# ifftshift of an 8192 x 8192 matrix: copies as pairs of half rows instead of blocks of half rows

## The chip, the cores and the metric

The kernel runs on one core of one Trainium2 chip. The metric is the device time of one execution in microseconds (us), lower is better; the figure for a kernel is the median of its runs.

## The reference

```python
def setup_inputs():
    return {"x": np.random.randn(8192, 8192).astype(np.float32)}

def reference(x):
    return np.fft.ifftshift(x)
```

For even sizes this swaps the halves of both axes: output row r, left half, is input row (r + 4096) mod 8192, right half; output row r, right half, is the left half of the same input row. Nothing is computed. 268.44 MB (8192 x 8192 x 4 bytes) are read and as many are written.

## The kernel before

Input and output lie in DRAM, and each transfer goes from the one straight to the other; no on-chip memory and no compute engine takes part. A row is 32 KB (R = C = 8192, float32), half a row 16 KB; `hr` and `hc` are 4096.

The helper `copy` (L26) starts one transfer on a queue (L29). Its list `dims` holds step and count of each dimension and is used for both sides, so source and destination have the same shape; the source is the destination shifted by half the rows and half the columns. The first dimension, of size 16, is divided over the 16 DMA engines.

There are two queues. SP (`nc.sync`) copies the left halves of output rows, ACT (`nc.scalar`) the right halves. Rows are taken in blocks of `rows` = 256: one transfer is 256 half rows, 4 MB. The shape `back` (L45) gives each engine one of 16 neighbouring rows, and its next piece lies 16 rows earlier, so engine e takes rows e + 240, e + 224, and so on down to e of the block. The loop (L47) goes from the last 1024 rows to the first, four blocks at a time in descending order; in the same step ACT works two blocks (512 rows, 16 MB) away from SP.

Ahead of the loop ACT copies one band of 16 half rows, the last of its first block, in strips of 1024 columns (4 KB pieces, L36 to L42): three strips are each divided into a transfer of 14, 9 or 4 rows and one of the rest, the fourth is one transfer of 16 rows. ACT's first block leaves this band out (`rest`, 240 half rows).

In all 71 transfers: 32 on SP, 39 on ACT. Their order on each queue is the program's. Eight semaphores serve in turn for the completion of all transfers, so the issue of a transfer waits until the one that had its semaphore has landed.

Of the kernel before, what the change touches and what calls it, by code (L numbers as in the profile page):

```python
# [1 line left out]

# [4 lines left out]


ENGINES = 16


@with_exitstack
def kernel(
    ctx: ExitStack,
    tc: tile.TileContext,
    x: bass.AP,
    out: bass.AP,
):
    nc = tc.nc
    R, C = x.shape  # L20
    hr = R // 2
    hc = C // 2
    per = 16
    rows = ENGINES * per

    def copy(queue, row, col, dims):  # L26

        src = (row + hr) % R * C + (col + hc) % C
        queue.dma_start(  # L29
            out=bass.AP(out.tensor, out.offset + row * C + col, dims),  # L30
            in_=bass.AP(x.tensor, x.offset + src, dims),
        )

    start = R - 3 * rows  # L36
    strip = hc // 4
    for n, k in enumerate((14, 9, 4)):
        col = hc + n * strip
        copy(nc.scalar, start + rows - ENGINES, col, [[C, k], [1, strip]])  # L40
        copy(nc.scalar, start + rows - ENGINES + k, col, [[C, ENGINES - k], [1, strip]])
    copy(nc.scalar, start + rows - ENGINES, hc + 3 * strip, [[C, ENGINES], [1, strip]])  # L42


    back = [[C, ENGINES], [-ENGINES * C, per], [1, hc]]  # L45
    rest = [[C, ENGINES], [-ENGINES * C, per - 1], [1, hc]]
    for first in range(R - 4 * rows, -1, -4 * rows):  # L47
        for n in (3, 2, 1, 0):
            copy(nc.sync, first + n * rows + rows - ENGINES, 0, back)
            right = first + (n + 2) % 4 * rows  # L50
            if right == start:
                copy(nc.scalar, right + rows - 2 * ENGINES, hc, rest)
            else:
                copy(nc.scalar, right + rows - ENGINES, hc, back)


# [1 line left out]
_INS = ['x']  # L58
_OUTS = [((8192, 8192), 'float32')]


# [23 lines left out]
```

## Time and profile before

| | |
|---|---|
| median of 3 runs | 821.84 us (821.51 to 823.76) |
| profiled execution: span from first to last instruction | 810.9 us |
| profiled execution: its own total | not given by the page; the median is 10.9 us over the span |
| copied | 268.44 MB, mean 331 GB/s; read and written 662 GB/s |
| packets | 17,520, of which 1,152 are under 8 KB |
| transfers on SP | 32 of 4096 KB |
| transfers on ACT | 31 of 4096 KB, 1 of 3840 KB, 7 strips of 8 to 64 KB |
| issue of one transfer on its queue | 571 ns (SP), 578 ns (ACT), medians |

How to read it: the page has a row for the busy share of the 16 DMA engines in 40 equal slices and one for the rate in each (GB/s counts bytes copied once; memory sees each twice). A packet is one piece of a transfer on one engine. q1 is SP's queue and q10 ACT's. The compute engines do nothing but four small constants at the start, so the chain of waits, which follows instructions, says nothing about this kernel; what there is to see is in the DMA rows.

### The profile page before, as it was taken

What the parts mean: (1) busy time and instruction counts of PE and PEld (TensorE: products, weight loads), DVE (VectorE), ACT (ScalarE), POOL (GpSimd) and SP (SyncE); (2) the same over time, 40 slices, a digit from 0 to 9 for tenths busy, and PEclk for the clock granted to TensorE, in tenths of its full rate; (3) what the DMA queues carried; (4) which work ended last, traced back from release to release, by engine and by line L of the source; (5) the groups of instructions that cost most, each with busy time, mean ns of one, the idle gap of its engine ahead of it and who ended that gap; (6) DMA issues with size and microseconds to landing.
All of it is one profiled execution on the core that took longest, in us unless ns stands there. A gap on an engine that the chain in (4) does not pass through costs nothing. (4 is left out here: it accounts for less than half of the span.)

```text
span 810.9 us, 116 instructions
## 1 busy us (share of the span) xinstructions
POOL 0.2 (0%) x4
## 2 busy tenths in 40 slices
POOL 0000000000000000000000000000000000000000
DMA  9999999999999999999999999999999999999998
GB/s 302 328 335 329 334 333 331 331 335 330 326 331 329 331 335 330 332 332 337 335 336 333 333 337 330 334 335 331 336 331 333 335 334 335 333 330 336 333 338 296
DMA packets 17520, 268.44 MB, mean 331 GB/s; under 512 B 1088, under 2 KB 1088, under 8 KB 1152
## 3 DMA queue, kind: packets, MB, share of 16 engines
q1 hardware_dynamic: 8704, 134.22, 49.7%
q10 hardware_dynamic: 8816, 134.22, 49.6%
HBM read 268.44 MB, written 268.44 MB: 662 GB/s over the span
## 5 line engine op out<-in xcount | busy, mean ns | idle before, releaser
L69 POOL MEMSET const-bfloat16-1.0<- 128x1 bf16 x1 | 0.1, 102 | 0.0
L69 POOL MEMSET const-uint8-127<- 128x1 uint8 x1 | 0.1, 102 | 0.0
L69 POOL MEMSET const-float32-0.0<- 128x1 f32 x1 | 0.1, 99 | 0.2 <-issue 0.2
L69 POOL MEMSET const-float32-1.0<- 128x1 f32 x1 | 0.1, 99 | 0.0
## 6 DMA issues: line engine op xcount, KB each, us to landing
out_dram<-in_x_dram SPq DMA_DIRECT2D x32, 4096.0 KB, 100.9
out_dram<-in_x_dram ACTq DMA_DIRECT2D x31, 4096.0 KB
out_dram<-in_x_dram ACTq DMA_DIRECT2D x1, 3840.0 KB
out_dram<-in_x_dram ACTq DMA_DIRECT2D x1, 64.0 KB, 10.8
out_dram<-in_x_dram ACTq DMA_DIRECT2D x1, 56.0 KB
out_dram<-in_x_dram ACTq DMA_DIRECT2D x1, 48.0 KB
out_dram<-in_x_dram ACTq DMA_DIRECT2D x1, 36.0 KB
out_dram<-in_x_dram ACTq DMA_DIRECT2D x1, 28.0 KB
```

The costliest lines, as they stand in the source:

```text
L69: nc = _bacc.Bacc("TRN2", target_bir_lowering=False, num_devices=1)
```

## The change

The left half of an output row comes from the right half of an input row, and the left half of the next input row goes to the right half of the next output row. In the input these two halves lie next to each other. `pair_copy` copies n such pairs: the source is one contiguous run of n x 32 KB that starts in the middle of input row k, and the destination is, for each pair, the left half of output row k + 4096 and the right half of the row below it. Of 256 pairs each of the 16 engines gets 16, 512 KB of the input in one run, written in pieces of 16 KB. Rows ascend.

SP copies the pairs that start in input rows 0 to 4095, ACT those of rows 4096 to 8191. The last pairs of each half would wrap around; so each queue starts with a shorter transfer of 240 pairs (rows 3840 to 4079 of its half) and three small ones by `half_copy`: 16 left halves, 15 right halves and one right half. Then 15 transfers of 256 pairs (8 MB) follow on each queue. That makes 38 transfers in place of 71. Strips, descending order and the distance of two blocks between the queues go.

```diff
-    def copy(queue, row, col, dims):
+    def pair_copy(queue, k, n):
+        to = (k + hr) % R
+        queue.dma_start(
+            out=bass.AP(out.tensor, out.offset + to * C, [[C, n], [C + hc, 2], [1, hc]]),
+            in_=bass.AP(x.tensor, x.offset + k * C + hc, [[C, n], [1, C]]),
+        )
 
+    def half_copy(queue, row, col, n):
         src = (row + hr) % R * C + (col + hc) % C
         queue.dma_start(
-            out=bass.AP(out.tensor, out.offset + row * C + col, dims),
-            in_=bass.AP(x.tensor, x.offset + src, dims),
+            out=bass.AP(out.tensor, out.offset + row * C + col, [[C, n], [1, hc]]),
+            in_=bass.AP(x.tensor, x.offset + src, [[C, n], [1, hc]]),
         )
 
+    full = hr // pairs - 1
+    last = full * pairs
+    n = hr - ENGINES - last
+    for queue, base in ((nc.sync, 0), (nc.scalar, hr)):
+        pair_copy(queue, base + last, n)
-    start = R - 3 * rows
-    ...
-    back = [[C, ENGINES], [-ENGINES * C, per], [1, hc]]
-    rest = [[C, ENGINES], [-ENGINES * C, per - 1], [1, hc]]
-    for first in range(R - 4 * rows, -1, -4 * rows):
-        ...
+        k = base + last + n
+        to = (k + hr) % R
+        half_copy(queue, to, 0, ENGINES)
+        half_copy(queue, to + 1, hc, ENGINES - 1)
+        half_copy(queue, (base + hr) % R, hc, 1)
+    for i in range(full):
+        pair_copy(nc.sync, i * pairs, pairs)
+        pair_copy(nc.scalar, hr + i * pairs, pairs)
```

(`pairs` is 256, as `rows` was.)

More of the change, by code (lines that the diff above doesn't have):

```diff
@@ L23 @@
     per = 16
-    rows = ENGINES * per
-    def copy(queue, row, col, dims):
+    pairs = ENGINES * per
+    def pair_copy(queue, k, n):
[5 more added lines that the diff above has]
+    def half_copy(queue, row, col, n):
         src = (row + hr) % R * C + (col + hc) % C
         queue.dma_start(
-            out=bass.AP(out.tensor, out.offset + row * C + col, dims),
-            in_=bass.AP(x.tensor, x.offset + src, dims),
-        )
-    start = R - 3 * rows
[L37 to L42, printed above, removed]
-    back = [[C, ENGINES], [-ENGINES * C, per], [1, hc]]
-    rest = [[C, ENGINES], [-ENGINES * C, per - 1], [1, hc]]
-    for first in range(R - 4 * rows, -1, -4 * rows):
[L48 to L54, printed above, removed]
+            out=bass.AP(out.tensor, out.offset + row * C + col, [[C, n], [1, hc]]),
+            in_=bass.AP(x.tensor, x.offset + src, [[C, n], [1, hc]]),
+        )
+    full = hr // pairs - 1
[11 more added lines that the diff above has]
+        pair_copy(nc.scalar, hr + i * pairs, pairs)
 _INS = ['x']
```

## The prediction

> **What bounds the kernel now.** The kernel has no arithmetic: it is 71 transfers from one DRAM tensor to another. So I read, in this order, the slices of the page, the DMA queues, the waits of the queue SP, and then my own table of stretches.
>
> The page first. The row DMA is the busy share of the 16 DMA engines in tenths for each fortieth of the span (20.3 us), and GB/s is what they copied.
>
> ```profile
> DMA  9999999999999999999999999999999999999998
> GB/s 302 328 335 329 334 333 331 331 335 330 326 331 329 331 335 330 332 332 337 335 336 333 333 337 330 334 335 331 336 331 333 335 334 335 333 330 336 333 338 296
> DMA packets 17520, 268.44 MB, mean 331 GB/s; under 512 B 1088, under 2 KB 1088, under 8 KB 1152
> q1 hardware_dynamic: 8704, 134.22, 49.7%
> q10 hardware_dynamic: 8816, 134.22, 49.6%
> HBM read 268.44 MB, written 268.44 MB: 662 GB/s over the span
> ```
>
> The engines are never free between head and tail: the two queues (q1 and q10, 134.22 MB each) fill 99.3% of them. So the time is packets x time per packet / 16. Of q1's 8,704 packets 512 are the completion marks of its 32 transfers (16 each, 9 ns apiece), so 8,192 carry 16 KB, and each takes 0.497 x 16 x 810.9 us / 8,192 = 787 ns. The single packet records say the same (mean 786, median 725), and they have a floor: the shortest is 608 ns, and 35% end within 620. An engine alone would thus need 608; the other 179 ns of the mean is waiting on memory, in some packets and not in others. That is the only thing this change can move: no byte goes away.
>
> Next, whether issuing or waiting costs anything. In the waits of the queue SP the columns are total us, times and longest us.
>
> ```profile
> SPq L29 <- DMA out_dram<-in_x_dram: 686.8, 28, 28.4
> SPq L80 <- DMA out_dram<-in_x_dram: 103.2, 3, 83.6
> out_dram<-in_x_dram SPq DMA_DIRECT2D x32, 4096.0 KB, 100.9
> ```
>
> SP waits nearly all the time, but for a completion mark of a transfer four back: a 4 MB transfer lands 100.9 us after its issue, which is 8 of them in flight (8 x 4.19 MB / 331 GB/s = 101 us). The rings hold work while SP waits, so the wait costs nothing.
>
> Last, the stretches (columns: window, its us, POOL, clock, DMA share, GB/s).
>
> ```profile
> 0.00:2.30 2.30, 0.20 (x4) 1.00 0.26 64
> 2.30:8.00 5.70, 0.00 (x0) 1.00 1.00 356
> 8.00:19.00 11.00, 0.00 (x0) 1.00 0.98 322
> 19.00:21.50 2.50, 0.00 (x0) 1.00 1.05 315
> 55.00:400.00 345.00, 0.00 (x0) 1.00 1.00 331
> 400.00:780.00 380.00, 0.00 (x0) 1.00 1.00 334
> 806.00:811.00 5.00, 0.00 (x0) 1.00 0.48 167
> ```
>
> From 2.3 to 8 us nearly all traffic is SP's and goes at 356; once both queues mix it is 331 to 334. So with the engines full throughout, the rate still moves by 7% with which addresses are in flight together: that is the size of what is at stake here. Between 18.8 us (SP's first transfer has landed) and about 21 (its second, issued at 19.25, is moving) only ACT's ring has work, and the engines stay full: one queue covers the other.
>
> The span is 810.9 us; the page gives no total for its execution, and the median of the runs is 821.84. I take the 10.9 us between them as fixed work around the span and add it to every figure below. About 0.3% (2.5 us) is what can be told from no change.
>
> **The change, part by part.**
>
> *Fewer, larger transfers.* 71 issues become 38 (30 of 8 MB, two of 7.5 MB, six small). An issue takes 0.57 us on its queue, 18.8 us on SP in all, beside full rings: nothing, covered by the 8 transfers in flight. If the cover were missing it would be one issue, 0.6 us.
>
> *The head.* ACT's seven strip transfers go, whose 4 KB packets held ACT's first large transfer back until some 13 us. SP's ring covered that (356 GB/s), so nothing is gained there; the 2.3 us before the first traffic stay.
>
> *The seam near 50 us.* This is new. With eight completion marks shared in turn, as the waits of before show, the first large transfers have to wait for the two 7.5 MB ones. Those land together: 7.86 MB at half of 331 GB/s is 47.5 us, from 2.3 on, so at 50. Behind them each ring has only its small pieces, about 2 packets an engine and queue: 4 x 787 ns = 3.1 us of cover. Restarting takes 0.5 us from landing to issue (18.8 to 19.25 above) and about 1.6 from issue to traffic (0.73 to 2.3), together 2.1; the 16 engines' marks of one transfer are spread over 1.2 to 2.7 us, so an engine that ended early runs dry for up to 3.1 - 2.1 against that spread, some 0 to 1.7 us. Bounds 0 and 4 (no cover, both rings); I take 1.
>
> *The tail and the split.* Each queue still moves 134.22 MB. The 15-row piece gives one engine a packet less per queue, the one-row piece may give another one more: at most 2 x 787 ns = 1.6 us late at one engine. Before has the like (its strips give engine 0 28 KB and engine 15 4 KB). Bounds -1 and +1.6; I take 0, since packets shift between engines' ends by about as much anyway.
>
> *Read runs of 32 KB or more instead of 16.* If a packet's own overhead were what counts, it would be seen at the floor: 16,384 B in 608 ns is 26.9 GB/s; a 4 KB strip packet takes 159 ns at the least, 25.8 GB/s. From the two, the fixed part of a packet is 159 - (608 - 159) / 3 = 9 ns, 1.2%, and only a packet that is at the floor gains it. Bounds: 0, and the fixed part of every packet, 16,368 x 9 ns / 16 = 9 us to the good; I take 0, since the engine isn't what the mean waits for.
>
> *The addresses in flight.* This is the term that decides. Before, an engine takes half a row and steps back 16 rows; the 16 engines stand on 16 neighbouring rows, 32 KB apart. SP and ACT work 512 rows (16 MB) apart. After, an engine walks its own 16 rows and the engines stand 512 KB apart; SP reads input rows from k and writes output rows from k + 4096 while ACT reads from k + 4096 and writes from k, so all four streams stand at the same row within a half, where before SP's two and ACT's two were 16 MB from each other. For it: a read run covers whole rows, and the writes of two halves of one output row follow each other. Against it: wider equal strides and four streams in step. No row of the trace shows a stride of 512 KB between engines, so I bound it. Better end: the stretch at 356 GB/s. Worse end: the first packet of each of the 16 engines, which start in step, takes 974 ns in the mean against 786 (it holds first-access delay as well). The nearest rows are whole slices, where the mixture of addresses turns as the rows advance: 326 to 338 in the 38 inner slices. I take the slow end, 326, because of the strides and because two mixed queues already cost 7% against one: 810.9 x 331 / 326 = 823.3.
>
> The Trainium skill has a rule that speaks against this part: DMA: Bandwidth & Descriptors, section Latency and other measured facts, gives copies between DRAM tensors whose rows lie at large powers of two apart, 207 GB/s at 512 KiB against 214 unhampered, and 164 and 103 at wider pitches. By its 512 KiB row an estimate would be 810.9 x 214 / 207 = 838.3, so 850 in all instead of 835; its pitch is between neighbouring 16 KiB rows, here it is between engines, and no run yet shows which counts.
>
> Sum: 823.3 + 1 + 0 + 10.9 = **835 us**.
>
> **The rivals.**
>
> *Slower, forecast (0.43).* As summed; with slices of 331 and 322 GB/s as its limits, 825 to 845.
>
> *Faster (0.31).* The whole-row reads and the paired half-row writes find memory better: the packets between 620 and 1,000 ns go towards the floor. Place: every packet after 2.3 us. At the best inner slice, 338 GB/s: 810.9 x 331 / 338 = 794.1, + 11.9 = 806. At 356: 766. It decides as soon as the mean packet falls under 783 ns per 16 KB, half a per cent below now, more than the seam costs. For it: 179 ns of waiting per packet is there to win, and the head runs at 356. Against it: the engines wander apart by 1 to 3 us, so which rows neighbour in time is partly chance, and longer runs need not matter.
>
> A ceiling for this case stands in the Trainium skill, HBM Reference, Specifications: about 716 GB/s for a domain. Against the page's 662 it would allow an estimate of 810.9 x 662 / 716 = 749.7, 762 in all; the stretch at 356 (712 read and written) agrees with it.
>
> *No change (0.11).* The pattern doesn't matter, the engines' wandering mixes it in both kernels: 821.84 + 1 = 823, between 819.4 and 824.3.
>
> *Much slower (0.12).* The strides alias: engines and streams that hit the same part of memory hold each other up all the time, not in turns. Slowest 2 us piece of the head after the strips (14 to 16 us): 299 GB/s; 810.9 x 331 / 299 = 897.7, so 910; at 974 ns a packet 1,016. Against it: continuous rings let a delayed engine fall out of step.
>
> *The split isn't what it says (0.03).* A contiguous source could be cut over fewer than 16 engines. With 15 for all: 810.9 x 16 / 15 = 865, so 877; fewer give more.
>
> **How the numbers follow.** The likeliest case gives 835. The range is 798 to 885: it holds the forecast, no change and the split at 15; of the faster case it leaves out the part under 798 (about 0.08), of the two bad ones what lies above 885 (about 0.10). The forecast's own range is 825 to 845. Slower by over 0.3%: 0.43 + 0.12 + 0.03 = 0.58; same 0.11; faster 0.31.
>
> **What would show it.** Forecast right: the inner slices near 326 GB/s, DMA still all 9, the two queues' shares still near 49.7% each. Faster: slices of 335 and above, more packets near the floor. Seam: a dip in the slice of 40 to 61 us, and a DMA share under 1 near 50 us; if several us are lost there, my cover is wrong. Much slower: slices under 310. A split over fewer engines: the DMA share at or under 0.94. The prediction is wrong if the slices rise above 331, or fall under 310.

## The result and the profile after

The changed kernel takes 862.8 us (median of 4 runs, 861.92 to 865.76) against 821.67 for the kernel before (4 runs): a ratio of 1.050, 95% interval 1.047 to 1.054, or 41 us. The forecast was 835 us.

The page of the changed kernel, in the rows that were read before:

```profile
span 864.0 us, 83 instructions
...
DMA  9999999999999999999999999999999999999998
GB/s 291 315 315 313 312 306 313 310 320 313 309 313 313 314 303 309 317 307 313 310 306 315 319 314 313 306 312 318 316 304 313 312 313 313 315 307 313 318 315 272
DMA packets 17020, 268.44 MB, mean 311 GB/s; under 512 B 606, under 2 KB 638, under 8 KB 638
...
q1 hardware_dynamic: 8510, 134.22, 50.0%
q10 hardware_dynamic: 8510, 134.22, 49.4%
HBM read 268.44 MB, written 268.44 MB: 621 GB/s over the span
```

The engines are as full as before (nines in all slices but the last, the two queues 99.4%), so the source was not cut over fewer than 16 engines. But every inner slice is slow: 303 to 320 GB/s, where before had 326 to 338. The loss is spread evenly, so it isn't an event. The packets show that it is their length. 16,382 packets of 16 KB now last 838 ns in the mean against 786 (of 16,368): 838.4 x 16,382 / 16 - 786.5 x 16,368 / 16 = 54 us, which is the difference of the spans, 864.0 - 810.9 = 53. The floor is still 608 ns; only 27% of the packets end within 620 ns, 35% before. No packet grew: although the source is one unbroken run, each record still moves 16 KB.

One reading aid. In every later run the time is 1.7 to 2.0 us above its span (here 865.76 and 864.0). So the profiled execution of before, whose own time is not on record, probably took about 812.7 us, some 7 us less than the fastest timed run of that kernel. Of the 53 us between the two spans some 44 are the change's (865.8 against the median 821.7).

The stretches of the changed kernel (window, its us, POOL, clock, DMA share, GB/s), with the seam and the tail:

```profile
2.30:8.00 5.70, 0.00 (x0) 1.00 0.95 336
...
19.00:48.00 29.00, 0.00 (x0) 1.00 0.99 315
...
50.00:52.00 2.00, 0.00 (x0) 1.00 0.89 287
52.00:54.00 2.00, 0.00 (x0) 1.00 0.89 297
...
60.00:400.00 340.00, 0.00 (x0) 1.00 1.00 311
400.00:800.00 400.00, 0.00 (x0) 1.00 1.00 312
```

The waits of SP (total us, times, longest us) and the transfers (number, size, us to landing) show what stands behind the rows of 50 to 54 us:

```profile
SPq L31 <- DMA out_dram<-in_x_dram: 120.6, 15, 51.2
...
out_dram<-in_x_dram ACTq DMA_DIRECT2D x15, 8192.0 KB, 215.1
out_dram<-in_x_dram SPq DMA_DIRECT2D x15, 8192.0 KB, 214.8
out_dram<-in_x_dram ACTq DMA_DIRECT2D x1, 7680.0 KB, 50.1
out_dram<-in_x_dram SPq DMA_DIRECT2D x1, 7680.0 KB, 54.3
```

SP's longest wait is 51.2 us, for a transfer of 7.5 MB; from then on 8 transfers of 8 MB are in flight, and each lands 215 us after its issue (64 x 1.049 MB / 311 GB/s = 216). So the seam is there, but at a share of 0.89 it costs about 4 x 0.11 = 0.4 us. (Windows of 2 us scatter by about as much in the kernel before, 0.88 to 1.14, so this is a size and not a measurement.) The rest of the time simply passes at 311.

### The profile page after: what moved, and what is told of

It reads as the page before. It is cut to its first block, busy times and chain, and to the rows that moved or that the text cites. A ratio compares the mean times of both kernels' runs of the same rounds, so it can differ in the third digit from the quotient of the medians.

```text
span 864.0 us, 83 instructions
## 1 busy us (share of the span) xinstructions
POOL 0.2 (0%) x4
## 6 DMA issues: line engine op xcount, KB each, us to landing
out_dram<-in_x_dram ACTq DMA_DIRECT2D x1, 7680.0 KB, 50.1
out_dram<-in_x_dram SPq DMA_DIRECT2D x1, 7680.0 KB, 54.3
```

## The experiments

The theories at first: **S**, the 512 KB between neighbouring engines; **P**, the four streams of SP and ACT at the same row of a half; **H**, the order of half rows within an engine. By **run** or unbroken run is meant that each packet of an engine starts, on one side, where its last one ended. The cuts of code leave lines out; "..." marks where. "Ratio" is to the kernel before, measured on the same chip, with its 95% interval.

### One part of the change in the kernel before: engines on rows of their own

```diff
-    back = [[C, ENGINES], [-ENGINES * C, per], [1, hc]]
+    back = [[per * C, ENGINES], [C, per], [1, hc]]
...
```

(`rest` and the first rows of the transfers change to match; within a block the rows now ascend.)

> The kernel before, with one thing of the change: each engine walks 16 rows of its own (512 KB between the engines) instead of every sixteenth row (32 KB between them). No pairs, SP and ACT still 16 MB apart. Theory S, the distance between the engines makes the loss: 850 to 865 us. Theory P, the loss comes from SP's and ACT's four streams standing at the same row of a half: 820 to 826. Theory H, the order of the half rows within an engine (right, left, right) makes it: 820 to 826.

821.3 us, ratio 0.999 (0.998 to 1.000). Theory S in its plain form falls: engines 512 KB apart cost nothing when nothing else changes. The page's slices:

```profile
GB/s 296 326 332 325 328 332 335 326 328 326 332 328 329 328 328 330 333 328 332 313 331 330 327 333 332 332 323 329 332 330 328 332 324 332 334 329 325 332 327 294
```

### One part of the change in the kernel before: ACT in the other half of the rows

```diff
-    start = R - 3 * rows
+    start = hr - rows
...
-            right = first + (n + 2) % 4 * rows
+            right = (first + n * rows + hr) % R
```

> The kernel before, with ACT's right halves taken 4096 rows away from SP's left halves instead of 512, which puts four streams at the same row of a half, as in the changed kernel. The strips move with ACT's first block. Theory P: 845 to 865 us. Theories S and H: 819 to 826.

821.7 us, ratio 1.000 (0.999 to 1.001). Theory P falls for this kernel.

### The changed kernel with ACT's blocks turned

```diff
-        pair_copy(nc.scalar, hr + i * pairs, pairs)
+        pair_copy(nc.scalar, hr + (i + 7) % full * pairs, pairs)
```

> The changed kernel with ACT's large transfers turned by 7 of 15, so that ACT never works at the same row of its half as SP (7 or 8 blocks of 8 MB away). Theory P: 820 to 840 us. Theories S and H: 858 to 866.

858.8 us, ratio 1.046 (1.043 to 1.048). The interval meets that of the changed kernel; if the place of the four streams has a part in the loss, it is some 4 of 41 us.

### The changed kernel with 480 KB between the engines

```diff
-    per = 16
+    per = 15
```

> The changed kernel with 15 pairs an engine in each large transfer instead of 16, so the engines stand 480 KB apart, 15 rows and no power of two, and a transfer is 7.5 MB; everything else is as changed. Theory S, if it is the power of two that hurts: 820 to 830 us. Theory S, if it is the mere width of the distance: 855 to 865. Theories P and H: 858 to 866.

843.5 us, ratio 1.026 (1.024 to 1.028), between all the forecasts: the distance matters after all, if the other parts of the change are there, and 32 KB less of it takes away 19 of 41 us. So no one of S, P and H alone gives this loss.

### The pairs taken apart, all else as changed

```diff
-        queue.dma_start(...)
+        for row, col in ((to, 0), (to + 1, hc)):
+            queue.dma_start(
+                out=bass.AP(out.tensor, out.offset + row * C + col, [[C, n], [1, hc]]),
+                in_=bass.AP(x.tensor, x.offset + k * C + hc + (row - to) * hc, [[C, n], [1, hc]]),
+            )
```

> The changed kernel with each pair transfer taken apart into two of 4 MB, first all left halves, then all right halves of the same rows; engines, rows, order and the distance of SP and ACT stay. Theory H1, an engine that alternates between the two halves from packet to packet makes the loss: 819 to 827 us. Theory H2, reading one unbroken run of 512 KB makes it: 819 to 827. Theory H3, SP and ACT being at the same half at the same time makes it: 855 us or more, since here all streams are at the same half all the time.

822.7 us, ratio 1.001 (1.000 to 1.002): the whole loss is gone, with the engines still 512 KB apart, ascending rows, SP and ACT 4096 rows apart and both at the same half. H3 falls. What makes the loss lies in the pair, and not in the small pieces at the start, which this kernel has too.

### Runs on the write side

```diff
-            out=..., [[C, n], [C + hc, 2], [1, hc]]),   in_=..., [[C, n], [1, C]]),
+            out=..., [[C, n], [1, C]]),                 in_=..., [[C, n], [-hc, 2], [1, hc]]),
```

> The changed kernel turned round: each engine writes 512 KB in one run (whole output rows) and reads the two halves of the input row in exchanged order; no wrap-around, so the small pieces go. H1: 852 to 866 us, the alternation is still there. H2: 819 to 830, nothing is read in a long run now. H3: 852 to 866.

866.2 us, ratio 1.055 (1.053 to 1.057). So H2 falls, in its form that the run must be read: a run that is written loses as much. A loss of this size also needs neither the small pieces nor the seam: this kernel has neither.

### ACT begins with the other half

```diff
+            out=bass.AP(out.tensor, out.offset + to * C + hc, [[C, n], [-hc, 2], [1, hc]]),
+            in_=bass.AP(x.tensor, x.offset + k * C, [[C, n], [1, C]]),
```

(for ACT's large transfers; SP's stay.)

> The changed kernel, but ACT pairs the halves of one input row (reads the row from its beginning, writes the right half and then the left half of one output row), so that it begins with the other half than SP; ACT needs no small pieces then. H3: 820 to 835 us, the two queues stand at opposite halves as in the kernel before. H1 and H2: 855 to 866.

857.8 us, ratio 1.044 (1.042 to 1.046). Some 5 us better than the changed kernel, not the 28 to 43 of H3.

### The distance, by the pairs in a transfer

Four runs change `per` alone, and with it the distance between engines, the length of each engine's run (it ends where the next engine's begins) and the size of a transfer. Two theories are put against each other here: **D**, alternating halves cost where the engines stand far apart; **Q**, they cost only in large transfers with much in flight.

> The changed kernel with 2 pairs an engine in each transfer instead of 16: engines 64 KB apart, transfers of 1 MB, 254 of them. If the distance between engines works together with the pairing, and a narrow one is better: 825 to 845 us. If only a distance that is no power of two helps (as the run at 480 KB did by 19 us): 858 to 868. The marks of 224 more transfers are 224 x 16 x 9 ns / 16 = 2 us of it.

> The changed kernel with 4 pairs an engine: engines 128 KB apart, transfers of 2 MB. Theory D: 820 to 845 us, and not above the run at 256 KB. Theory Q: 820 to 826.

> The changed kernel with 8 pairs an engine: engines 256 KB apart, transfers of 4 MB as in the kernel before. Theory D: between 64 KB (no loss) and 512 KB (5%), 830 to 862 us. Theory Q: 4 MB transfers and 32 MB in flight as before, 820 to 830.

> The changed kernel with 32 pairs an engine: engines 1 MB apart, transfers of 16 MB. If 512 KB is a bound beyond which the distance costs: 858 us or more. If 512 KB is a special distance: 820 to 845.

| between engines | transfer | time, us | ratio (interval) |
|---|---|---|---|
| 64 KB | 1 MB | 822.9 | 1.001 (1.000 to 1.002) |
| 128 KB | 2 MB | 826.0 | 1.005 (1.003 to 1.007) |
| 256 KB | 4 MB | 825.7 | 1.006 (1.004 to 1.007) |
| 384 KB | 6 MB | 833.7 | 1.014 (1.011 to 1.016) |
| 480 KB | 7.5 MB | 843.5 | 1.026 (1.024 to 1.028) |
| 512 KB | 8 MB | 862.8 | 1.050 (1.047 to 1.054) |
| 1 MB | 16 MB | 1039.1 | 1.263 (1.255 to 1.270) |

(384 KB comes from a later run, below.) Up to 256 KB the cost is at most 0.6%, then it grows. The 825.7 us at 256 KB lie in Q's range and not in D's, so these runs alone do not speak for D; the twins below decide. The 822.9 us at 64 KB are a little better than forecast. The run at 1 MB holds a second answer. Its first transfers have 496 pairs, so for those the engines stand 31 rows, 992 KB, apart; the 1024 KB begin at about 104 us. Its stretches:

```profile
50.00:100.00 50.00, 0.00 (x0) 1.00 1.00 318
100.00:112.00 12.00, 0.00 (x0) 1.00 1.03 303
112.00:500.00 388.00, 0.00 (x0) 1.00 0.99 255
500.00:1000.00 500.00, 0.00 (x0) 1.00 1.00 253
```

The rate falls from 318 to 255 GB/s at the change from 992 to 1024 KB. At the same moment the large transfers in flight go from two to eight; but the run at 480 KB has the same step near 50 us without a change of distance, and there the rate doesn't fall:

```profile
19.00:48.00 29.00, 0.00 (x0) 1.00 0.99 316
60.00:400.00 340.00, 0.00 (x0) 1.00 1.00 321
```

The changed kernel, which goes from 480 to 512 KB at its seam, falls from 315 to 311 there. The run's length changes by only 3% from 992 to 1024 KB, so it is the distance that counts in this step. The inner slices of the run at 480 KB go at about the same rate as those at 992:

```profile
GB/s 292 318 314 321 324 317 319 314 325 327 318 324 326 321 317 321 315 321 320 331 319 320 316 315 324 317 321 324 321 324 320 323 316 323 312 324 322 323 321 277
```

So there are two terms: wide distances cost up to some 3% (318 to 321 GB/s, against 327 to 329 in the mean inner slice of the kernels that lose nothing), and exactly 512 KB and exactly 1 MB come on top, with 2.3% of the time (843.5 to 862.8 us) and 20% of the rate. Whether it is the power of two or any multiple of 512 KB is not shown: no run stands at 768 KB.

### Distance or size of the transfers: a pair of twins

Both kernels move one pair an engine in each transfer, 512 KB in all and 4 MB in flight. The distance differs, and with it the run: at 512 KB an engine's next transfer goes on where its last one ended, at 32 KB it jumps after every pair.

```diff
-            out=..., [[C, n], [C + hc, 2], [1, hc]]),        in_=..., [[C, n], [1, C]]),
+            out=..., [[step * C, 16], [C + hc, 2], [1, hc]]), in_=..., [[step * C, 16], [1, C]]),
...
```

`step` is 16 in the first (15 for the 240 odd pairs), 1 in the second.

> The changed kernel in transfers of one pair an engine (512 KB in all), with the engines still 512 KB apart: 16 such transfers cover the rows of one of 8 MB. The pairs, their order on each engine and the rows are as changed; only 4 MB are in flight at a time instead of 64. Theory D, alternation costs where the engines stand 512 KB apart: 855 to 868 us. Theory Q, it costs only in large transfers with much in flight, which let the engines run free: 820 to 830.

> As the run of small transfers with 512 KB between the engines, but with 32 KB between them (16 neighbouring rows in each transfer). Same transfers in number and size. Theory D: 820 to 828 us. Theory Q: the same as its twin, 820 to 830. If both are slow, small transfers cost by themselves.

874.6 us (ratio 1.065, 1.061 to 1.069) and 826.3 us (1.006, 1.004 to 1.008). The same number and size of transfers, 48 us apart: it is where the engines stand and walk, not the size of the transfers or how much is in flight. Q falls; the first twin even lies above D's range. Distance and run length can't be told apart by these two; the step from 992 to 1024 KB above does that. Of the 5 us that the second twin lies above the kernel before, about 4 are completion marks (8,255 short packets of 9 ns against 1,088, over 16 engines). Slices of the first and then of the second:

```profile
GB/s 279 291 303 309 306 312 312 308 312 309 312 310 315 307 306 310 313 315 312 309 311 309 315 309 315 309 313 309 308 312 304 316 314 306 318 309 309 309 315 273
```

```profile
GB/s 298 323 325 331 328 324 321 321 325 335 331 330 330 327 330 322 335 324 324 324 332 329 329 321 333 321 333 324 332 329 326 335 331 329 325 332 330 319 331 291
```

### Reads or writes

The twins, with the wide distance on one side only.

```diff
+            out=..., [[1 * C, 16], [C + hc, 2], [1, hc]]),   in_=..., [[step * C, 16], [1, C]]),
...
```

> Small transfers of one pair an engine, with the engines 512 KB apart in the input and 32 KB apart in the output (the rows of each block of 256 come out permuted, so this is not the reference's output; every byte is still moved once). Its two limits are the runs of small transfers with 512 KB on both sides (874.6 us) and 32 KB on both (826.3). If reads make the loss: 860 to 876. If writes make it: 823 to 835. If each side has its part: 835 to 860.

> The mirror image: engines 32 KB apart in the input and 512 KB apart in the output (rows permuted in each block of 256, not the reference's output). If writes make the loss: 860 to 876 us. If reads: 823 to 835. If each side has its part: 835 to 860.

850.4 us (ratio 1.037, 1.033 to 1.040) with wide reads, 832.3 us (1.014, 1.009 to 1.019) with wide writes. Above the narrow twin these are 24 and 6 us, together 30 of 48: each side has its part, that of the reads, which are the unbroken run here, is the larger, and the rest needs both. By the forecasts the first time says "each side" and the second, 832.3, "reads"; but its interval lies clear of the narrow twin's (1.004 to 1.008), so the writes' part is small and not nothing. In that kernel the reads run on for only one pair, 32 KB, so a wide distance costs a little even with runs that short.

### Alternating halves without an unbroken run

```diff
-            out=..., [[C, n], [C + hc, 2], [1, hc]]),      in_=..., [[C, n], [1, C]]),
+            out=..., [[C, n], [2 * C + hc, 2], [1, hc]]),  in_=..., [[C, n], [2 * C - hc, 2], [1, hc]]),
...
```

(The small pieces change to match.)

> The changed kernel with the two halves of a pair two rows apart instead of adjoining: right half of input row k, left half of row k + 2. Engines still 512 KB apart and alternating halves, but neither side is one unbroken run. Theory U, the unbroken run on one side is needed for the loss: 819 to 828 us. Theory A, the alternation of halves is enough: 853 to 868.

823.0 us, ratio 1.002 (1.000 to 1.003). Theory A falls and U stands: an engine that alternates between right and left halves loses nothing, if the halves aren't neighbours. Between this kernel and the changed one lies one row in the address of each second packet, and 40 us. Its slices (of an execution of 828.0 us, the slowest of its ten):

```profile
GB/s 304 318 325 323 324 332 323 328 324 330 327 328 329 329 327 330 324 329 327 328 328 321 332 331 325 329 328 328 325 326 329 322 328 328 332 324 328 329 324 269
```

### The wide distance without runs, and 384 KB

Two last runs: the pairs taken apart with `per = 32`, and the changed kernel with `per = 12`.

> The pairs taken apart (first left halves, then right halves) and 32 rows an engine: engines 1 MB apart, no unbroken run, transfers of 8 MB. If the unbroken run is needed for the loss at any distance: 820 to 830 us. If 1 MB hurts by itself: 860 to 1040.

> The changed kernel with 12 pairs an engine: engines 384 KB apart. If the loss grows steadily with the distance, it lies between the runs at 256 KB (825.7 us) and 480 KB (843.5): 830 to 840. If multiples of a large power of two count (384 KB is 3 x 128 KB, 480 KB is 15 x 32 KB): at or above 843. If a distance must pass some bound: 823 to 828.

At 1 MB without the unbroken run: 822.0 us, ratio 1.000 (0.999 to 1.001), where the same distance with runs takes 1039. So the run is needed at 1 MB too. (The packet records hold no addresses: that each engine takes a block of neighbouring rows is read from the shapes. The runs bear it out where the distance is written out as a dimension of 16: 821.3 us without runs and 874.6 with them, both at 512 KB. At 1 MB without runs it is not written out.) The slices:

```profile
GB/s 301 331 325 328 332 325 330 333 333 329 326 330 332 329 330 321 330 330 333 323 328 330 324 335 331 333 326 328 334 329 327 328 331 329 323 330 334 332 326 289
```

At 384 KB: 833.7 us, within the forecast of a loss that grows with the distance.

No kernel of these beats the one before by more than can be measured. Six lie between 821.3 and 823.0 us (engines on no unbroken run, or 64 KB apart), three more at 826 (engines 128 or 256 KB apart, or small transfers with 32 KB).

## Why the prediction was wrong, and where it was right

**What bounds the kernel: right.** The engines are full in every run, and nearly all of the differences, from 821 to 1039 us, is in the mean length of a packet of 16 KB (786 ns in before, 794 in the run of engines on rows of their own, 838 after, 1001 at 1 MB).

**Fewer transfers, head, split and tail at nothing: right.** The runs at 64 KB (262 transfers) and with the pairs apart lie within 1.3 us of before.

**The seam at 1 us: right in place, a little high.** It is at 50 to 54 us, as worked out, and costs about 0.4 us. The two 7.5 MB transfers didn't land together, though: ACT's landed 50.1 us and SP's 54.3 us after the issue, so SP's ring still had work while ACT restarted.

**The addresses in flight: right in sign, mis-sized, and for the wrong reason.** This term was taken as 823.3 - 810.9 = 12.4 us, from the slowest whole slice of before, 326 GB/s. It measured about 41: the slices fell to 303 to 320, 311 in the mean. The step that failed is the price of this term, by the choice of its row. The slices of before vary as the mixture of the same kind of streams varies, and none of them holds engines that walk an unbroken run at a wide equal distance; they could bound nothing of that. The far row that I kept only for a rival, 299 GB/s, was a little nearer to 311 than the one I took, but that is luck: it doesn't hold the new pattern either.

**The reason given.** Two were named against the change, wide equal strides and four streams in step, and one for it, that a read run covers whole rows. The four streams are worth nothing in the kernel before and at most about 4 us here. The strides alone are worth nothing, at 512 KB or 1 MB. And the unbroken run, which I counted as the change's merit, is the half without which the strides are harmless. The forecast set the two against each other, as a merit and a cost; the runs show that they cost only together.

**The Trainium skill's rule.** The estimate from the Trainium skill (DMA: Bandwidth & Descriptors, section Latency and other measured facts) gave 850, nearer to 862.8 than the sum. Its direction agrees with the runs, a distance at a large power of two and a strong growth beyond it, and so in part does its remedy, a distance off the power (992 KB instead of 1024 gave 318 for 255 GB/s). But if its pitch is read as the distance between engines, the kernel of engines on rows of their own should have lost as well, and it measured 0.999. So the nearness of the 850 is partly luck.

**The rivals.** Faster: the packets near the floor became fewer, not more. Much slower through aliasing: equal strides that hold the engines up all the time fit what came, at a price between the forecast's and its own, though only together with runs, which it doesn't name; that the engines hit the same part of memory no run shows. At 1 MB its upper end of 1,016 us was passed. My argument against it, that a delayed engine falls out of step in continuous rings, was wrong: the loss lasts for the whole span.

**The sum** had a second slip that hardly told: by the estimate of 812.7 us above, the 10.9 us "around the span" were 1.8 us around it and some 9 by which that one execution was quicker than the median. Some small slips moved nothing: 331 GB/s gives 823 us for the forecast's lower limit, not 825; the shortest 4 KB packet took 156 ns, not 159; SP's issues take 18.6 us in all, not 18.8; and the piece of one row went out as 16 packets of 1 KB, not as one.

**Open.** Why an unbroken run is needed, and why exactly 512 KB and 1 MB cost more than 480 and 992, no run shows: none looks into the memory. A spread of the starting points over the engines was not tried, nor a long run with a narrow distance, which can't be had as long as each engine's run ends where the next one's begins.

## What to carry to other kernels

When 16 engines stream through DRAM, look at two things together: the distance between the engines' positions, and whether each engine walks an unbroken run. Here a wide distance without any adjoining packets is free (821 to 823 us), and runs with the engines 256 KB or less apart, which are also shorter runs, cost at most 0.6%; a wide distance and long runs together cost 5% at 512 KB and 26% at 1 MB. Longer contiguous runs per engine gained nothing here: the packets stayed at 16 KB, and their floor was the same 608 ns in both kernels. And where the trace of before doesn't hold the new access pattern, its slowest slice is no bound for it.

## What the runs showed of the hardware that was not expected

- 32 KB in the distance between engines, 992 against 1024 KB, moved the copy rate from 318 to 255 GB/s; from 480 to 512 KB the whole kernel went from 843.5 to 862.8 us.
- One row in the address of each second packet (left half of row k + 2 instead of k + 1) was worth 40 us.
- Patterns without runs take the same time whatever their order: ascending or descending rows, engines 32 KB or 1 MB apart without runs, SP and ACT 16 MB or 128 MB apart all take 821.3 to 823.0 us.
